# The start and the attention scores of a hybrid decoder trunk: loads, warm-up, split scores, and the place of the last projections

## The chip, the cores and the metric

The kernel runs on one core of a Trainium2 chip. The core has a matrix engine (TensorE, PE in the profile, with its weight loads listed as PEld), VectorE (DVE), ScalarE (ACT), GpSimd (POOL), and a queue engine (SyncE, SP) that issues nearly all DMAs here. Each engine works through its own instructions strictly in the order in which the compiler put them. The metric is the device time of one execution in microseconds (us); lower is better.

## The reference

The input x is 512 tokens by 1024 channels, float32. Two layers follow, each a mixer and a squared-ReLU MLP, each with a residual and a layer norm. Only the mixer of layer 0 is touched by the change:

```python
h = x @ mix_w_in[i] + mix_b_in[i]                    # 1024 -> 2048
u, q, k, v = jnp.split(h, [512, 1024, 1536], axis=-1)
s5_out = s5_mixer(u, ...)                            # diagonal state-space scan, then gelu and a GLU
sb_out = stick_breaking_attention(q, k, v)           # 8 heads of 64, strictly causal
mix = jnp.concatenate([s5_out, sb_out], axis=-1) @ mix_w_out[i] + mix_b_out[i]
...
z = jnp.einsum('bqhd,bkhd->bhqk', q_blk, kf) * scale           # scale = 1/8
log_beta = jax.nn.log_sigmoid(z)
log_keep = jnp.where(strict, jax.nn.log_sigmoid(-z), 0.0)
after = lax.cumsum(log_keep, axis=3, reverse=True) - log_keep
weights = jnp.where(strict, jnp.exp(log_beta + after), 0.0)
out = jnp.einsum('bhqk,bkhd->bqhd', weights, vf)
```

## The kernel before

**Numbers.** Products of weights and activations keep float32 accuracy with operands split in two: hi is the value rounded to F32R, lo is the rest, and `gemm` (L190) forms hi·hi, hi·lo and lo·hi as three F32R products into one PSUM bank. `split` (L185) makes hi with a ScalarE copy and lo with a VectorE subtraction. Some products are still plain F32: the S5 ones, the attention scores (L602) and the weighted sum over the values (L635).

**Weights.** `Weights` (L51) streams 512 KB units: `fetch` issues the load on the SP queue into one of two raw buffers, `_prep` splits the unit into hi (ScalarE, L84) and lo (VectorE, L85) in one of three slots. `next` hands the next unit to a product and splits up to two ahead. The units are listed in the order in which `ORDER` (L48) uses them.

**The start.** The eight 128-channel pieces of x are loaded first (L248), then two weight units (u0 and u1), then the raw S5 tables Braw and Craw and the bias rows. PE first transposes the S5 parameters (`parp`, L276), then each piece of x (L286, four transposes a piece). Each piece is split (`x0h`, `x0l`), and GpSimd adds the halves back to make the residual X (L289). `FIRST` (L45) says behind which pieces the first two weight units are split. Then u0, the first 128 channels of u, is projected by 24 products (L536); eight transposes of Craw (`cp`, L542) are ordered behind its last product; u1 to u3 follow.

**The mixer.** What follows is emitted by the words of `ORDER`: `q0` to `q3` project q, k and v of a pair of heads (`qkv`, L562); `s0` to `s3` build and scan a quarter of the S5 states (`s5_states`, L457); `y0` to `y3` form their outputs; `a0` to `a3` are the attentions of the four pairs; then `gelu` (with a way through DRAM and back, `yf`) and `glu` with its products gg and gv. Last comes `accum` (products acmo, L707), the first half of the output projection. The four sine and cosine tables of the S5 scan (L419 to L435) are all made ahead of `s0`.

**One attention** (L576): v is transposed; the scores of a head stand in three groups A, B and C of key blocks, each in a PSUM bank tagged z (four banks, shared with the S5 products); softplus is Abs, Exp and Ln on ScalarE and one VectorE step, then a GpSimd mask and a split; products with a triangle of ones (L626) sum along the keys; Exp, a mask and the product with v end it. Projections and glu use another three banks (`mm`). The query is scaled by 1/8 when it is copied out of PSUM.

**What sets the order.** The program text gives each instruction a priority (earlier text first, `high_priority` ahead of all), and the compiler's list scheduler puts an engine's instructions in order: in its own simulated time it takes, of those whose operands and buffers are there, the one of best priority. So a projection fills holes of an attention that stands ahead of it in `ORDER`. `add_manual_dep` with NOSYNC and `issue_after` fix an order on one engine without a semaphore. ScalarE's function tables are loaded by `Act` (L116) in the order of the text: a new set is loaded only behind all functions of the old one.

Of the kernel before, what the change touches and what calls it, by code (L numbers as in the profile page):

```python
# [9 lines left out]
F32 = mybir.dt.float32  # L10
F32R = mybir.dt.float32r
# [33 lines left out]
FIRST = (4, 7)  # L45
ATT = "sB0 sC0 wB0 sA0 wC0 sB1 sC1 wB1 sA1 wC1 wA1 wA0"
MIX_BUFS = (3, 4, 1, 4, 3)
ORDER = "q0 s0 q1 y0 s1 a0 y1 s2 q2 y2 s3 a1 y3 gelu q3 a2 glu a3".split()  # L48


class Weights:  # L51
# [23 lines left out]
    def _prep(self, n):  # L75
        nc = self.nc
        while self.done < min(n, len(self.units)):
# [6 lines left out]
            i0 = nc.scalar.copy(hi, raw).ins  # L84
            i1 = nc.vector.tensor_sub(lo, raw, hi.bitcast(F32)).ins  # L85
# [4 lines left out]
            self.done += 1  # L90

# [45 lines left out]
def kernel(ctx: ExitStack, tc: tile.TileContext, a: dict, out: bass.AP):  # L137
# [71 lines left out]
    for o in ORDER:  # L209
        if o[0] == "q":  # L210
            for s in range(1, 4):
                units += units_of("qkv", w_in, 0, 8, [512 * s + 128 * int(o[1])], 128)
# [12 lines left out]
    def zz(name):  # L225
        return psum("z", name, MIX_BUFS[1])
# [16 lines left out]

    xin = []
    with tc.high_priority():
        for j in range(KT):
            xt = att.tile([P, 4, P], F32, tag=("spt", "wt", "q", "k")[j % 4], name=f"xin{j}", bufs=(MIX_BUFS[3], MIX_BUFS[4], 2, 2)[j % 4])
            nc.sync.dma_start(xt, a["x"][0][:, P * j : P * (j + 1)].rearrange("(b p) f -> p b f", p=P))  # L248
            xin.append(xt)
    W = Weights(tc, 2)  # L250
    W.add_slots(wpool, 3)
    W.raw, W.units = s5, units
    W.fetch(0)
# [21 lines left out]
    parp = zz("parp")  # L275
    PE.transpose(parp[:, :96], nat, ident[:96, :96])  # L276
    PE.transpose(parp[:, 96:112], brow, ident[:16, :16])
    par = s5.tile([P, 96], F32, tag="par", name="par")
    V.tensor_copy(par, parp[:, :96])
    V.tensor_copy(PB, parp[:, 96:112])  # L280
    V.tensor_scalar(bq8, PB[:, 4:8], 0.125, None, op0=ALU.mult)
    xs, order = [], []
    for j in range(KT):
        ps = (mm if j % 2 else s5ps)(f"xT{j}")
        for b in range(4):
            PE.transpose(ps[:, b * P : (b + 1) * P], xin[j][:, b, :], ident)  # L286
        xh, xl = page(f"x0h{j}"), page(f"x0l{j}")
        order.append(split(xh, xl, ps))
        G.tensor_tensor(X[j], xh.bitcast(F32), xl.bitcast(F32), op=ALU.add)  # L289
        xs.append((xh, xl))  # L290
    for i, j in enumerate(FIRST):
        W.fence = order[j]
        W._prep(i + 1)
# [126 lines left out]
    for q in range(4):  # L420
# [10 lines left out]
        tc_, ts_ = spage(f"tc{q}", "tabc", 4), spage(f"ts{q}", "tabs", 4)  # L431
# [3 lines left out]
        tabs.append((tc_, ts_))  # L435

# [98 lines left out]
    u0 = mm("u0")  # L535
    u0_last = gemm(u0, W.next(), slice(0, P), xs, 0, T)  # L536
# [25 lines left out]
    def qkv(p):  # L562
        r = []
        for s, n in enumerate("qkv"):
            ps, b = in_proj(4 + 4 * s + p, f"{n}{p}")
            t_ = att.tile([P, T], F32, tag=n, name=f"{n}{p}")
            if s == 0:
                act(t_, ps, AF.Identity, bias=bq8[:, p : p + 1], scale=0.125)
            else:
                act(t_, ps, AF.Identity, bias=b)  # L570
# [569 lines left out]
```

## Time and profile before

| | |
|---|---|
| median of three runs | 1252.57 us (1252.2 to 1254.42) |
| the profiled execution's own time | 1254.81 us |
| its span in the trace | 1252.8 us |
| mean granted PE clock | 0.984 |
| PE busy | 1199.8 us of the span |
| VectorE, ScalarE, GpSimd busy | 778.4, 562.2, 124.3 us |
| first product of u0, first product of u1 | 14.10 us, 23.57 us |
| last product of the mixer (acmo) | 268.38 us |

Times in the rows of the profile count from the span's start. A row of the order of time has the start, the duration, the engine, the line of the kernel, the operation, the tile written and the tiles read, the shape and the count, and, in brackets, the idle time before it with what ended it. A PE record is longer than the distance to the next product, because products are pipelined.

### The profile page before, as it was taken

What the parts mean: (1) busy time and instruction counts of PE and PEld (TensorE: products, weight loads), DVE (VectorE), ACT (ScalarE), POOL (GpSimd) and SP (SyncE); (2) the same over time, 40 slices, a digit from 0 to 9 for tenths busy, and PEclk for the clock granted to TensorE, in tenths of its full rate; (3) what the DMA queues carried; (4) which work ended last, traced back from release to release, by engine and by line L of the source; (5) the groups of instructions that cost most, each with busy time, mean ns of one, the idle gap of its engine ahead of it and who ended that gap; (6) DMA issues with size and microseconds to landing.
All of it is one profiled execution on the core that took longest, in us unless ns stands there. A gap on an engine that the chain in (4) does not pass through costs nothing.

```text
span 1252.8 us, 16561 instructions
## 1 busy us (share of the span) xinstructions
PE 1199.8 (96%) x6503; PEld 1011.9 (81%) x6503; DVE 778.4 (62%) x1313; ACT 562.2 (45%) x1012; POOL 124.3 (10%) x153
## 2 busy tenths in 40 slices
PE   7999989999999999999999999789899999999997
PEld 5886756688988888888998889689898888888885
DVE  8985954567833434434378999999862442444446
ACT  4944476633622313313346576886462331323230
POOL 4002021113000000000030011213500000000000
PEclk9999998999999999999999999889899999999999
DMA  7620121151532222333223221004052242323211
GB/s 183 172 63 17 52 65 45 43 170 32 169 101 101 90 87 92 102 101 101 72 69 102 68 68 35 1 1 135 4 177 90 69 133 67 108 77 118 84 51 68
DMA packets 111662, 105.93 MB, mean 85 GB/s; under 512 B 9378, under 2 KB 99746, under 8 KB 111584
## 3 DMA queue, kind: packets, MB, share of 16 engines
q1 hardware_dynamic: 111424, 104.84, 27.0%
q8 instruction: 51, 0.84, 0.3%
q14 instruction: 27, 0.22, 0.1%
q10 hardware_dynamic: 160, 0.03, 0.0%
HBM read 100.66 MB, written 4.19 MB: 84 GB/s over the span
## 4 chain that ended last, share of the span: by engine, by line
PE 77%; DVE 14%; ACT 5%; issue 1%; POOL 1%; DMA 1%; SPq 0%; DVEq 0%; ACTq 0%; POOLq 0%
PE f L196 23%; PE g L1070 11%; PE acf L196 10%; PE fl L196 4%; PE tlb L196 3%; PE h L1054 3%; DVE cz L312 3%; PE tld L196 3%; PE cv L969 2%; DVE cy L312 2%; PE av L635 2%; DVE wlo L85 2%; PE pl L196 1%; PE q L196 1%; PE acmo L196 1%
## 5 line engine op out<-in xcount | busy, mean ns | idle before, releaser
L84 ACT CAST whi<-raw 128x1024 fp32r<-128x1024 f32 x180 | 188.1, 1049 | 414.3 <-PE f L196 109.4
L85 DVE TENSOR_TENSOR wlo<-raw,whi 128x1024 fp32r<-128x1024 f32 x180 | 226.2, 1260 | 222.8 <-ACT whi L84 222.5
L1070 PE MATMUL g<-whi,hh 128*128 128x512 f32 x208 | 81.5, 392 | 0.0
L1070 PE MATMUL g<-wlo,hh 128*128 128x512 f32 x208 | 81.5, 392 | 0.0
L1070 PE MATMUL g<-whi,hl 128*128 128x512 f32 x208 | 81.4, 391 | 0.0
L196 PE MATMUL f<-xdh,whi 128*128 128x512 f32 x208 | 80.9, 389 | 0.0
L196 PE MATMUL f<-xah,whi 128*128 128x512 f32 x208 | 80.9, 389 | 0.0
L196 PE MATMUL f<-xal,whi 128*128 128x512 f32 x208 | 80.9, 389 | 0.0
L196 PE MATMUL f<-xdh,wlo 128*128 128x512 f32 x208 | 80.9, 389 | 0.0
L196 PE MATMUL f<-xdl,whi 128*128 128x512 f32 x208 | 80.9, 389 | 0.0
L196 PE MATMUL f<-xah,wlo 128*128 128x512 f32 x208 | 80.9, 389 | 0.0
L196 PE MATMUL acf<-hl,whi 128*128 128x512 f32 x192 | 75.2, 392 | 0.0
L196 PE MATMUL acf<-hh,whi 128*128 128x512 f32 x192 | 74.9, 390 | 0.0
L196 PE MATMUL acf<-hh,wlo 128*128 128x512 f32 x192 | 74.7, 389 | 0.0
L186 ACT CAST hh<-fr 128x512 fp32r<-128x512 f32 x64 | 39.7, 621 | 71.6 <-DVE fr L308 71.6
L187 DVE TENSOR_TENSOR hl<-fr,hh 128x512 fp32r<-128x512 f32 x64 | 44.2, 692 | 37.3 <-ACT hh L186 37.3
L312 DVE SCALAR_TENSOR_TENSOR cy<-hp,wdw,cy 128x512 f32<-128x512 f32 (+1 forms) x91 | 60.6, 675 | 0.1
L312 DVE SCALAR_TENSOR_TENSOR cz<-hp,wdw,cz 128x512 f32<-128x512 f32 (+1 forms) x86 | 60.0, 702 | 0.0
L969 PE MATMUL cv<-hph,dh 128*128 128x256 f32 (+1 forms) x113 | 39.9, 353 | 10.3 <-ACT hph L186 8.6
L308 DVE TENSOR_TENSOR fr<-fr 128x512 f32<-128x512 f32 x64 | 43.8, 686 | 5.4 <-ACT fr L125 5.4
L1070 PEld LDWEIGHTS g<-whi,hl 128*128 128x128 f32 x208 | 39.1, 188 | 8.6
L1070 PEld LDWEIGHTS g<-wlo,hh 128*128 128x128 f32 x208 | 39.1, 188 | 8.6
(624 smaller groups left out, 3158.3 us busy)
## 6 DMA issues: line engine op xcount, KB each, us to landing
raw<-in_ffn_w_dram SPq DMA_DIRECT2D x48, 1024.0 KB, 5.2
raw<-in_ffn_w_dram SPq DMA_DIRECT2D x32, 512.0 KB, 3.6
raw<-in_conv_w_pw_dram SPq DMA_DIRECT2D x12, 1024.0 KB, 5.8
raw<-in_mix_w_in_dram SPq DMA_DIRECT2D x16, 512.0 KB, 4.1
xin<-in_x_dram SPq DMA_DIRECT2D x8, 256.0 KB, 4.4
raw<-in_s_w_glu_dram SPq DMA_DIRECT2D x4, 512.0 KB, 3.4
raw<-in_mix_w_out_dram SPq DMA_DIRECT2D x4, 512.0 KB, 3.8
raw<-in_mix_w_out_dram SPq DMA_DIRECT2D x2, 1024.0 KB, 6.2
```

Source lines behind the costliest of these rows:

```text
L84: i0 = nc.scalar.copy(hi, raw).ins
L85: i1 = nc.vector.tensor_sub(lo, raw, hi.bitcast(F32)).ins
L186: i0 = S.copy(hi, src).ins
L187: i1 = V.tensor_sub(lo, src, hi.bitcast(F32)).ins
L196: ins = PE.matmul(ps[:, c0:c1], u[:, k, ksl], v[:, c0:c1], start=start and k == 0 and i == 0, stop=stop and k == n - 1 and i == 2).ins
L308: V.tensor_tensor(o, x, y, op=op)
L312: V.scalar_tensor_tensor(o, x, s, y, op0=op0, op1=op1)
L635: PE.matmul(av[R, P * kb :], vt[:, kb, R], w_[:, o : o + T - P * kb], start=summed[h] == 1, stop=summed[h] == 4, skip_group_check=True)
L969: PE.matmul(cps[j][:, c0:c1], u, v[:, t + c0 : t + c1], start=t == 0 and i == 0, stop=t == n - 1 and i == 2)
L1054: PE.matmul(ps, u, v, start=k == 0 and i == 0, stop=k == nk - 1 and i == 2)
L1070: PE.matmul(pss[b], u, v[:, kk, :], start=k + kk == 0 and i == 0, stop=k + kk == nb - 1 and i == 2)
```

## The change

1. *Loads.* The first weight unit is issued ahead of x; the pieces of x use other buffers.
2. *Warm-up.* 24 transposes of the identity matrix (`WARM`) run on PE ahead of the first piece of x, into the bank of the attention output.
3. *First products.* u0 is no longer projected after all transposes: the three products of piece k are placed behind the transposes of piece k+2. The first weight unit is split with the first piece, the next two behind the last piece. The S5 parameter transposes move behind those of the third piece.
4. *Residual.* X is copied from the transposed PSUM bank by ScalarE; GpSimd no longer adds the halves.
5. *Scores.* q and k are kept as hi and lo, and a score block is three F32R products. The factor 1/8 moves into the split of the q weights. q has two buffers of each half, k one (`QK_BUFS`); before, both had two.
6. *Tables.* The fourth sine table is made behind `y0`, and three buffers hold the tables instead of four.
7. *Order.* `a2` stands ahead of `q3`.

```diff
-FIRST = (4, 7)
+WARM = 24
+QK_BUFS = (2, 1)
-ORDER = "q0 s0 q1 y0 s1 a0 y1 s2 q2 y2 s3 a1 y3 gelu q3 a2 glu a3".split()
+ORDER = "q0 s0 q1 y0 t3 s1 a0 y1 s2 q2 y2 s3 a1 y3 gelu a2 q3 glu a3".split()
...
+            if key[0] == "q":
+                i0 = nc.scalar.mul(hi, raw, 0.125).ins
+                i1 = nc.vector.scalar_tensor_tensor(lo, raw, 0.125, hi.bitcast(F32), op0=ALU.mult, op1=ALU.subtract).ins
...
+    def first(self):
+        self._prep(1)
+        self.got += 1
+        return self.ready.pop(0)
...
+    with tc.high_priority():
+        W.fetch(0)
     xin = []
     with tc.high_priority():
         for j in range(KT):
...
+            tag, bufs = (("spt", MIX_BUFS[3]), ("wt", MIX_BUFS[4]), ("qh", QK_BUFS[0]))[(0, 1, 0, 1, 0, 1, 0, 2)[j]]
...
-    W.fetch(0)
     W.fetch(1)
...
+    warm = psum("av", "warm", MIX_BUFS[2])
+    for i in range(WARM):
+        ready = PE.transpose(warm[:, :P], ident, ident).ins
+    xs, w0, u0 = [], None, mm("u0")
+    def u0_part(k, after):
+        xh, xl = xs[k]
+        for i, (u, v) in enumerate(((w0[0], xh), (w0[0], xl), (w0[1], xh))):
+            ins = PE.matmul(u0, u[:, k], v, start=k == 0 and i == 0, stop=k == KT - 1 and i == 2).ins
+            tc.add_manual_dep(ins, after, NOSYNC, reason="order of the first products")
+            after = ins.name
+        return ins
+    u0_last = ready
     for j in range(KT):
...
+            ins = PE.transpose(ps[:, b * P : (b + 1) * P], xin[j][:, b, :], ident).ins
+            if j == 0 or j > 2:
+                tc.add_manual_dep(ins, u0_last.name, NOSYNC, reason="order of the first products")
         xh, xl = page(f"x0h{j}"), page(f"x0l{j}")
-        order.append(split(xh, xl, ps))
-        G.tensor_tensor(X[j], xh.bitcast(F32), xl.bitcast(F32), op=ALU.add)
+        with tc.high_priority():
+            W.fence = split(xh, xl, ps)
+            if j == 0:
+                W.fence = None
+                w0 = W.first()
+        S.copy(X[j], ps)
         xs.append((xh, xl))
+        if j > 1:
+            u0_last = u0_part(j - 2, ins.name)
+        if j == 2:
+            parp = zz("parp")
...
+    for k in (KT - 2, KT - 1):
+        u0_last = u0_part(k, u0_last.name)
+    W.prep_to(3)
     W.fence = None
...
-    u0 = mm("u0")
-    u0_last = gemm(u0, W.next(), slice(0, P), xs, 0, T)
...
+                t_ = tuple(att.tile([P, T], F32R, tag=n + x, name=f"{n}{x}{p}", bufs=QK_BUFS[s]) for x in "hl")
+                act(t_[0], ps, AF.Identity, bias=b)
+                stt(t_[1], ps, b, t_[0].bitcast(F32), ALU.add, ALU.subtract)
...
-                ins = PE.matmul(z[:, o : o + T - P * kb], k_[R, P * kb : P * kb + P], q_[R, P * kb :], start=o == 0,
-                                stop=True, skip_group_check=True).ins
+                for i, (u, v) in enumerate(((0, 0), (0, 1), (1, 0))):
+                    ins = PE.matmul(z[:, o : o + T - P * kb], k_[u][R, P * kb : P * kb + P], q_[v][R, P * kb :],
+                                    start=o == 0 and i == 0, stop=i == 2, skip_group_check=True).ins
...
+        elif o[0] == "t":
+            tables(int(o[1]))
```

More of the change, by code (lines that the diff above doesn't have):

```diff
@@ L83, in _prep @@
             lo = pool.tile([P, nk, ncol], F32R, tag=f"wlo{s}", name=f"wlo{self.done}", bufs=1)
-            i0 = nc.scalar.copy(hi, raw).ins
-            i1 = nc.vector.tensor_sub(lo, raw, hi.bitcast(F32)).ins
+            if key[0] == "q":
+                i0 = nc.scalar.mul(hi, raw, 0.125).ins
+                i1 = nc.vector.scalar_tensor_tensor(lo, raw, 0.125, hi.bitcast(F32), op0=ALU.mult, op1=ALU.subtract).ins
+            else:
+                i0 = nc.scalar.copy(hi, raw).ins
+                i1 = nc.vector.tensor_sub(lo, raw, hi.bitcast(F32)).ins
             if self.fence:
@@ L419, with tables @@
     tabs = []
-    for q in range(4):
+    def tables(q):
         fa, fb, fr = spage(f"fa{q}"), spage(f"fb{q}"), spage(f"fr{q}")
@@ L435 @@
         tabs.append((tc_, ts_))
+    for q in range(3):
+        tables(q)
     Gx = s5.tile([P, 2, 4, 4, 2, 16], F32, tag="Gx", name="Gx")
```

45 lines of the change are left out of this document (20 added, 25 removed).

## The prediction

> **What bounds the kernel now.** I read the page's busy shares first, then ten-microsecond windows of the mixer stage, then the order of time where a window was poor.
>
> ```profile
> span 1252.8 us, 16561 instructions
> PE 1199.8 (96%) x6503; PEld 1011.9 (81%) x6503; DVE 778.4 (62%) x1313; ACT 562.2 (45%) x1012; POOL 124.3 (10%) x153
> ```
>
> TensorE (PE) is busy for 96% of the span, so time is won only where it has a hole, runs at a low clock, or is given less to do. The diff touches nothing behind the last product of the first mixer:
>
> ```profile
> 268.38 0.39 PE L196 MATMUL acmo<-gh,wlo 128*128 128x512 f32 x1
> ```
>
> Whatever it wins must be won before 268.4 us; the stages behind it move along unchanged.
>
> ```profile
> 10.00:20.00 10.00, 6.75 (x31) 5.28 (x30) 9.93 (x15) 4.56 (x8) 9.29 (x9) 0.85 0.89 175
> 40.00:50.00 10.00, 9.81 (x44) 7.94 (x43) 9.91 (x30) 9.80 (x19) 0.00 (x0) 1.00 0.59 182
> 100.00:110.00 10.00, 8.66 (x34) 5.05 (x34) 5.87 (x12) 5.25 (x12) 1.91 (x4) 0.83 0.15 45
> 140.00:150.00 10.00, 9.70 (x109) 7.39 (x108) 9.85 (x20) 4.95 (x10) 0.00 (x0) 1.00 0.17 55
> 180.00:190.00 10.00, 5.77 (x24) 3.81 (x22) 5.67 (x10) 9.29 (x18) 0.70 (x2) 0.89 0.56 165
> 190.00:200.00 10.00, 10.00 (x42) 8.46 (x42) 4.33 (x7) 4.87 (x11) 1.82 (x4) 0.77 0.37 99
> ```
>
> The columns are the stretch, then busy time of PE, its weight loads, VectorE (DVE), ScalarE (ACT), GpSimd (POOL), the granted clock, DMA share and GB/s. PE has two poor places: the start, and 180 to 190 us, behind which the clock is 0.77. VectorE is full at 40 and at 140 us, so a cost there is not free, and has room at 100.
>
> **Start.** All loads go out on one queue, x ahead of the weights:
>
> ```profile
> 0.80 5.34 SPq L248 DMA_DIRECT2D xin<-in_x_dram  x8
> 13.00 1.04 ACT L84 CAST whi<-raw 128x1024 fp32r<-128x1024 f32 x1 [1.63 <-DMA raw<-in_mix_w_in_dram]
> 18.75 0.63 PE L196 MATMUL u<-x0l,whi 128*128 128x512 f32 x1
> 19.17 0.63 PE L196 MATMUL u<-x0h,wlo 128*128 128x512 f32 x1
> 22.55 0.39 PE L196 MATMUL u<-x0h,wlo 128*128 128x512 f32 x1
> 22.78 1.03 PE L542 MATMUL cp<-ident,Craw 128*128 128x128 f32 x8
> 23.57 0.48 PE L196 MATMUL u<-x0h,whi 128*128 128x512 f32 x1
> 18.00:20.00 2.00, 2.00 (x6) 1.56 (x5) 1.97 (x3) 0.00 (x0) 2.00 (x3) 0.50 0.68 151
> L186 ACT CAST x0h<-xT 128x512 fp32r<-128x512 f32 x8 | 4.4, 588 | 3.8 <-PE xT L286 3.8
> L187 DVE TENSOR_TENSOR x0l<-xT,x0h 128x512 fp32r<-128x512 f32 x8 | 5.1, 678 | 0.0
> L473 ACT COPY gt<-gp 128x512 f32<-128x512 f32 x8 | 4.3, 590 | 9.4 <-PE gp L471 9.4
> ```
>
> Before, the ninth load (the first weights) has landed at 13.00; only then do the 24 products of u0 begin, part of them at a clock of 0.50 (0.42 us apart instead of 0.23), and u1 begins at 23.57. After, the same nine loads run with the weights first, so the last piece of x is there at about 13.0, the bytes being equal. Behind it: four transposes (0.11 each by the 8 in 1.03) 0.45, x0h 0.59, x0l 0.68, handovers about 0.4, the last three products 0.69: 15.8. ACT now also copies each piece to X, 0.59 by the nearest row, so a piece costs it two spacings of about 0.52; the loads spread evenly from 0.8 to 13.0 put the first piece near 5, so eight pieces and one weight split (1.04) end near 14.4, and PE's 1.14 a piece near 14.2, both just in time. I allow 0.6 of lag: u0 ends near 16.4. Then cp (0.8) and u1, whose weights want 1.04 on ACT behind the last x0h and 1.2 on VectorE: 17.3 to 18. I take 18.0 against 23.57: **-5.5**; bounds -7 (no ACT lag) and -1 (first rival). On the queue the first weights now stand ahead of x, and the second weights where they stood. PE's transposes of piece j+2 stand ahead of the products of piece j, so a late piece holds up two pieces' products; with pieces landing some 1.2 apart that is hidden. The parameter transposes (two, 0.7 in all) move behind the third piece, so VectorE's small-step chain starts some 2 us later than before, and gains that back below: 0. The 24 warm-up transposes lie in PE's empty first 6 us, their PSUM bank is not needed before the first attention: 0.
>
> POOL's eight additions to X go. They slow VectorE beside them:
>
> ```profile
> 15.02 5.83 POOL L289 TENSOR_TENSOR X<-x0h,x0l 128x512 f32<-128x512 f32 x4
> 17.71 1.94 DVE L312 SCALAR_TENSOR_TENSOR sm<-sm,sm 128x16 f32<-128x16 f32 x2
> 22.23 0.17 DVE L312 SCALAR_TENSOR_TENSOR sm<-sm,sm 128x16 f32<-128x16 f32 x1
> 19.57 2.36 DVE L85 TENSOR_TENSOR wlo<-raw,whi 128x1024 fp32r<-128x1024 f32 x1
> 24.28 1.22 DVE L85 TENSOR_TENSOR wlo<-raw,whi 128x1024 fp32r<-128x1024 f32 x1 [0.92 <-ACT whi L84]
> ```
>
> A 0.17 us step takes about 1, a 1.22 us one 2.36. Without them VectorE runs some 5 us ahead there. PE, not VectorE, is what later steps wait for up to 90 us, so I count 0, but it is why VectorE follows an earlier start.
>
> **Rounded scores.** A score block was one F32 product (two passes in the trace); now it is three F32R products.
>
> ```profile
> 239.16 0.70 PE L602 MATMUL z3C<-q,k 64*128 64x256 f32 x2
> 241.74 1.12 PE L602 MATMUL z3A<-q,k 64*128 64x512 f32 x2
> 181.25 1.13 PE L602 MATMUL z2B<-q,k 64*128 64x384 f32 x4
> L312 DVE SCALAR_TENSOR_TENSOR yl<-yf,yh 128x512 fp32r<-128x512 f32 x4 | 3.0, 741 | 0.7 <-ACT yh L125 0.6
> ```
>
> A single product's record outlasts its spacing by 0.16 (0.39 against 0.23). So A took 0.96, C 0.54, B 0.97; three passes at 0.227 per 512 columns are 0.68, 0.34, 0.68: -0.28, -0.20, -0.29, twice per attention, -1.5 at most, less where two heads' blocks already ran side by side. In the last two attentions PE is filled with other products and I count -1.4 and -1.1; in the first two the ACT and POOL chain sets the pace: 0. Sum **-2.5**, bounds -5 and +1 (three 64-row weight loads in place of two, 0.1 each where exposed). The low halves are eight more VectorE instructions, 0.74 each by the nearest row, 5.9 in all. For pairs 1 to 3 they can run only when the attention before has released the tiles, behind the first and second attentions' scores, where VectorE has holes; 0, and the third rival if not. ScalarE writes the high halves in the place of the F32 copies: 0. The scaling of the q weights keeps its instruction count: 0. With one k buffer a finished k waits in its PSUM bank until the attention before has made its last scores, which leaves two banks for projections; the copy that waits holds up what stands behind it on ScalarE, the next attention's exponentials at worst, but it is placed behind those scores, which come first on PE too: 0, with the +2 of the next part as its far end. The fourth sine table moves behind y0: on ScalarE and VectorE its 16 instructions need the buffer that the first S5 group gives back, and the first attention's exponentials wait for its sines through the table order. The VectorE steps, by the 0.69 and less of such 512-column work some 2.5 us, fit the hole there,
>
> ```profile
> 79.26 1.23 DVE L85 TENSOR_TENSOR wlo<-raw,whi 128x1024 fp32r<-128x1024 f32 x1 [3.62 <-ACT whi L84]
> ```
>
> 0 again; if the hole is gone, up to +2.5.
>
> **q3 behind the third attention.** The hole it could fill:
>
> ```profile
> 176.28 1.12 DVE L312 SCALAR_TENSOR_TENSOR U<-U,par,yp 128x128 f32<-128x128 f32 x4 [4.79 <-PE yp L523]
> 177.17 0.50 PE L196 MATMUL v<-x0h,whi 128*128 128x512 f32 x1
> 182.22 0.62 ACT L131 ACTIVATE g<-g 128x512 f32<-128x512 f32 x1
> 183.83 1.28 ACT L127 ACT_TABLE_LOAD   x1
> 188.73 0.79 PE L196 MATMUL gg<-yh,whi 128*128 128x512 f32 x1 [4.23 <-ACT yh L125]
> ```
>
> PE waits 4.23 for gelu's result, then runs at a low clock: by the means of 0.89 and 0.77 in the two windows above that costs some 3 more. But the third attention's exponentials need the table load at 183.83, which the code puts behind gelu's last tanh (182.22), and that hangs on the S5 output at 176.28. Putting the attention's scores ahead of v3's products (177.17) starts none of that earlier; the work that is ready before 188 is the same. v3 will also start later, for want of a bank, and so lie in the hole rather than ahead of it. I count half of the clock loss, **-1.5**; bounds -7.2 (hole and clock both gone) and +2 (v3's products wait and displace others).
>
> **Sum:** -5.5 - 2.5 - 1.5 = -9.5. The profiled execution took 1254.81, 2.2 above the median of the runs, so 1245.3 by it, and 1243 against the median of 1252.57.
>
> **The rivals.**
> 1. *The start is lost again.* cp stands behind u0 on PE in program order and needs Craw:
>
> ```profile
> L542 PEldq EVENT_SEMAPHORE  x2: 51/51/51, 17.8 to 19.8; - x2
> ```
>
> Its loads landed by 19.8. If cp is still placed ahead of u1, PE stands from 16.4 to 20 or later and then runs at half clock, as at 18 us above: the start is worth 1 to 2, the sum about -5: 1247.5. Against it: the order is worked out anew and could put u1 first.
> The same end by a page: the Trainium skill, "TensorE: Matmul & The Clock Gate", Part 4 (PE-mode transpose), says that transposes do not count as PE work for the clock, so that the warm-up would do nothing. The trace speaks against that: with nothing but transposes on PE, they went from 7 to 10 in a microsecond.
>
> ```profile
> 8.00:9.00 1.00, 1.00 (x7) 1.00 1.16 310
> 10.00:11.00 1.00, 1.00 (x10) 1.00 1.18 289
> ```
>
> As a mechanism of this kernel: 24 first products 0.42 apart instead of 0.23 cost 4.6 and leave the start about -1, the same 1247.5.
> 2. *The hole closes too.* The attention's scores and v3 interleave so that PE never stands long enough to lose its clock: 5.7 more than the 1.5 counted at most, about -5 more: 1238. The chain through tanh speaks against it.
> 3. *VectorE decides* (the other side). If its full stretches (40 and 140 us above) set the end of the stage, the earlier start is worth nothing and the 5.9 of low halves are paid: +5.9 - 2.5 = +3.4, 1256. It decides once VectorE's last S5 state sum ends no earlier than before. Against it: up to 95 us PE waits for VectorE once,
>
> ```profile
> PE u L196 <- DVE wlo L85: 1.2, 1, 1.2
> ```
>
> and VectorE has the holes at 76 to 79 and at 100 us.
> 4. *Given back at the hole.* The chain to gelu does not move with the start, since it also hangs on lock-ups such as
>
> ```profile
> 157.27 5.68 POOL L595 TENSOR_SCALAR_AFFINE_SELECT sp1B<-sp1B 128x256 f32<-128x256 f32 x1 [0.30 <-DVE sp1B L312]
> ```
>
> and the hole grows by what the start won: about -1.5, 1251.
>
> **How the numbers follow.** Chances: forecast 0.45, rival 1 0.22, rival 2 0.16, rival 3 0.10, rival 4 0.07. Two parts in a thousand, 2.5 us, is what a measurement of this kernel can tell: faster 0.83, same 0.07, slower 0.10. The range 1234 to 1252 takes in the forecast with its unknown costs and the first two rivals and most of the fourth; it leaves out the third and the far end of the second. The forecast's own range is 1238 to 1247.
>
> **What would show it.** u0's last product near 16.4 and u1 near 18 with the clock at 1.00 throughout; VectorE steps of 0.17, not 1, there; cp without a wait. Three score products 0.23 apart. The mixer's last product near 259 instead of 268.4. The wait of gg for yh, if under 4 us, and the clock behind it. Wrong: cp waiting for Craw, a clock of 0.50 in the first products, a wait of a PSUM bank ahead of v3 or gg, the S5 sums ending at 155 as before.

## The result, and the profile after

The changed kernel takes 1259.6 us in the median of its runs, the old one beside it 1254.23: a ratio of 1.0049, 95% interval 1.0031 to 1.0066, so 5.4 us slower by the medians. The prediction was 1243, in a range of 1234 to 1252. All times below are such medians, and all ratios are to the old kernel run beside them; the profiled executions of one kernel scatter by a few us around the median, so single traces are read for places, not for the total.

The page of the changed kernel, span and busy shares:

```profile
span 1255.9 us, 16680 instructions
PE 1203.1 (96%) x6559; PEld 1017.5 (81%) x6559; DVE 777.0 (62%) x1321; ACT 565.1 (45%) x1020; POOL 111.5 (9%) x145
```

TensorE's share is the same, its busy time 3.3 us longer. The order of time on TensorE at the start, and the mixer's last product:

```profile
16.37 0.39 PE L298 MATMUL u<-x0h,wlo 128*128 128x512 f32 x1
18.44 0.63 PE L582 MATMUL cp<-ident,Craw 128*128 128x128 f32 x4 [1.69 <-DMA Craw<-in_s_c_re_dram]
21.15 1.08 PE L582 MATMUL cp<-ident,Craw 128*128 128x128 f32 x4 [2.08 <-DMA Craw<-in_s_c_im_dram]
21.89 0.78 PE L206 MATMUL u<-x0h,whi 128*128 128x512 f32 x1
22.46 0.63 PE L206 MATMUL u<-x0l,whi 128*128 128x512 f32 x1
...
273.55 0.39 PE L206 MATMUL acmo<-gh,wlo 128*128 128x512 f32 x1
```

u0's last product starts at 16.37, just as worked out. Then TensorE stands twice for Craw, because cp comes before u1 in its order, and u1 starts at 21.89, its first products 0.43 apart instead of 0.23. The mixer's last product starts at 273.55; before it was 268.38.

ScalarE, the loads' queue and VectorE behind this, in the order of time (rows left out between them):

```profile
18.05 1.16 ACT L135 ACTIVATE ue<-u,PB 128x512 f32<-128x512 f32 x1
29.46 1.05 ACT L89 CAST whi<-raw 128x1024 fp32r<-128x1024 f32 x1 [10.26 <-DMA raw<-in_mix_w_in_dram]
30.42 0.21 ACT L141 ACTIVATE sm<-sm 128x16 f32<-128x16 f32 x1
...
25.39 1.02 SPq L67 DMA_DIRECT2D raw<-in_mix_w_in_dram  x2
...
30.55 1.23 DVE L90 TENSOR_TENSOR wlo<-raw,whi 128x1024 fp32r<-128x1024 f32 x1 [5.73 <-ACT whi L89]
```

This is the second loss, and the prediction had no line for it. The fourth weights are loaded only at 25.39, behind the bias rows (before, their load went out at 21.96, between the rows). Their high half is next in ScalarE's order, so ScalarE stands 10.26 us, and the small steps towards the sine tables (sm) stand behind it although their inputs are there. VectorE, next in whose order is the low half, stands too:

```profile
20.00:25.00 5.00, 3.85 (x11) 3.23 (x12) 2.87 (x21) 0.00 (x0) 0.00 (x0) 0.50 0.10 22
25.00:30.00 5.00, 5.00 (x20) 4.03 (x19) 0.00 (x0) 0.54 (x1) 0.00 (x0) 0.82 0.72 195
150.00:160.00 10.00, 7.63 (x38) 5.99 (x37) 10.00 (x17) 9.25 (x19) 3.39 (x4) 1.00 0.01 2
180.00:190.00 10.00, 7.26 (x39) 5.57 (x37) 6.96 (x13) 9.73 (x19) 0.65 (x2) 1.00 0.36 92
190.00:200.00 10.00, 7.82 (x33) 6.39 (x34) 4.31 (x8) 4.83 (x10) 0.70 (x2) 0.83 0.49 146
```

The columns are those of the prediction's windows. From 25 to 30 us VectorE does nothing at all. Further on, TensorE is busy 7.63 of the ten from 150 to 160 (9.19 before), and from 180 to 200 it does 15.08 where it did 15.77: the old hole in front of gg is not closed but split, as two waits of TensorE from 150 to 210 us show (total, times, longest):

```profile
PE gg L206 <- ACT yh L135: 2.2, 1, 2.2
PE z2B L670 <- ACT sh2B L196: 1.9, 1, 1.9
```

What is missing from 150 to 160 is told by the products of v for the fourth pair of heads (v3 in the prediction) between 140 and 200 us, first and last start, before (line 196) and after (line 206):

```profile
L196 PE MATMUL v<-x0h,whi x8: 387/391/499, 155.7 to 180.0; 128*128 128x512 f32 x8
...
L206 PE MATMUL v<-x0h,whi x8: 389/391/397, 168.7 to 186.0; 128*128 128x512 f32 x8
```

Before, v3 began at 155.7 and filled the gaps of the second attention. Now it begins at 168.7. Up to that attention's scores nothing is lost (147.7 now, 147.4 before): the whole loss of the mixer arises behind them. Some of the expectations below call this tile v2.

### The profile page after: what moved, and what is told of

Read it like the earlier page. It is cut to its first block, busy times and chain, and to the rows that moved or that the text cites. A ratio compares the mean times of both kernels' runs of the same rounds, so it can differ in the third digit from the quotient of the medians.

```text
span 1255.9 us, 16680 instructions
## 1 busy us (share of the span) xinstructions
PE 1203.1 (96%) x6559; PEld 1017.5 (81%) x6559; DVE 777.0 (62%) x1321; ACT 565.1 (45%) x1020; POOL 111.5 (9%) x145
## 4 chain that ended last, share of the span: by engine, by line
PE 71%; DVE 15%; issue 6%; ACT 4%; DMA 2%; SPq 1%; POOL 1%; DVEq 0%; POOLq 0%; ACTq 0%
PE f L206 23%; PE g L1116 11%; PE acf L206 10%; PE fl L206 4%; PE h L1100 3%; PE tld L206 3%; DVE cz L350 3%; PE tlb L206 2%; PE cv L1015 2%; DVE wlo L90 2%; DVE cy L350 2%; PE av L679 2%; PE acmo L206 1%; PE pl L206 1%; PE pv L206 1%
## 5 line engine op out<-in xcount | busy, mean ns | idle before, releaser
L89 ACT CAST whi<-raw 128x1024 fp32r<-128x1024 f32 x176 | 183.8, 1049 | 409.4 <-PE f L206 111.3
L90 DVE TENSOR_TENSOR wlo<-raw,whi 128x1024 fp32r<-128x1024 f32 x176 | 219.4, 1250 | 222.9 <-ACT whi L89 222.3
```

## The experiments

Each run's ratio is to the old kernel on the same chip; in the same terms the changed kernel stands at 1.0049 (1.0031 to 1.0066). Diffs are against the changed kernel unless another is named.

### First four: one part undone at a time

**cp behind u1.**

```diff
-    with tc.issue_after(u0_last):
-        for i in range(2):
-            cp = zz(f"cp{i}")
...
     for j in range(4):
         ps, b = in_proj(j, f"u{j}") if j else (u0, pv("mix_b_in", 0))
+        if j == 1:
+            with tc.issue_after(last[0]):          # u1's last product
+                for i in range(2):
+                    cp = zz(f"cp{i}")
...
```

> The changed kernel with one edit: the eight transposes of Craw (cp) are emitted behind u1's 24 products instead of ahead of them. Theory S (the start's gain is lost because cp, in its old place ahead of u1, waits on TensorE for Craw, which lands at about 21, and the clock then drops to half): u1's first product comes at 17.5 to 18.5 instead of 21.89, all its products are 0.23 apart, u1 ends near 24 instead of 29.8, and the kernel is 3 to 5.5 us faster than the changed one, near 1255. It can be cut to some 3 by the weights of u3, whose load is now issued only at 25.4, behind the bias rows. Rival (VectorE or the attention chain sets the pace of the stage): u1 comes as early, but the mixer's last product stays within 1 us of 273.5 and so does the time of 1259.6.

In this kernel the moved block's loop variable overwrote u1's bias, so u1 is computed with another bias; the work is the same. Measured: 1263.11, ratio 1.0074 (1.0059 to 1.0089), 3 us slower still. u1's first product came at 16.50 at full clock, as expected; but ScalarE's load wait stayed, at 30.23, and VectorE's waits (second row: total and longest) grew:

```profile
30.23 1.04 ACT L89 CAST whi<-raw 128x1024 fp32r<-128x1024 f32 x1 [8.56 <-DMA raw<-in_mix_w_in_dram]
...
DVE wlo L90 <- ACT whi L89: 10.4, 2, 8.3
```

The first S5 state Sx came at 74.1 instead of 71.7. Theory S alone falls: TensorE's early start runs into the missing weights, for which it now stood 2.27 us at 31.33.

**The old order.**

```diff
-ORDER = "... y3 gelu a2 q3 glu a3".split()
+ORDER = "... y3 gelu q3 a2 glu a3".split()
```

> The changed kernel with q3 put back ahead of a2 in ORDER, nothing else. Theory O (the swap costs: y3's products, the third attention and v3 fall behind each other from 160 us on, where the changed kernel falls from 0.5 to 3.5 us behind the old one): the third attention's sums and gg move back, gg's first product comes near 189.5 instead of 192.2, the mixer's last product at 270 to 271 instead of 273.5, and the kernel is 2 to 3.5 us faster, near 1256.5. Rival (the three passes of the scores and their low halves cost it, wherever q3 stands): the time stays within 1 us of 1259.6.

Measured: 1258.39, 1.0033 (1.0020 to 1.0045). 1 to 2 us faster, the intervals overlapping; the swap is not the main cost. gg's first product came later (194.6), not earlier, so the reason given was wrong too.

**The old start.** Loads, transposes, u0 and X as in the old kernel, with x's eight pieces in the buffers that the changed kernel leaves free.

```diff
-    with tc.high_priority():
-        W.fetch(0)
     xin = []
...
+    W.fetch(0)
     W.fetch(1)
...
-        S.copy(X[j], ps)
+        G.tensor_tensor(X[j], xh.bitcast(F32), xl.bitcast(F32), op=ALU.add)
...
-        if j > 1:
-            u0_last = u0_part(j - 2, ins.name)
...
+    u0 = mm("u0")
+    u0_last = gemm(u0, W.next(), slice(0, P), xs, 0, T)
```

> The changed kernel with the old start (x ahead of the weights on the queue, no warm-up transposes, u0 behind all transposes, X added on GpSimd), the rest of the change kept. Theory S (the new start as it stands is worth nothing): 1259 to 1260.5, u1's end within 1 us of the old 29.0. Rival (the new start wins 3 or more in VectorE's and GpSimd's work, which other parts then lose): 1262 or more. Other rival (the new start itself costs, through late loads): 1257 or less.

Measured: 1258.33, 1.0027 (1.0014 to 1.0040), in none of the three expected ranges, and u1's end at 27.1 instead of 29.0. The new start as built wins nothing; with overlapping intervals, it may cost up to 3.

**F32 scores.**

```diff
-                t_ = tuple(att.tile([P, T], F32R, tag=n + x, ..., bufs=QK_BUFS[s]) for x in "hl")
-                act(t_[0], ps, AF.Identity, bias=b)
-                stt(t_[1], ps, b, t_[0].bitcast(F32), ALU.add, ALU.subtract)
+            t_ = att.tile([P, T], F32, tag="qkv"[s] + ("h" if s == 0 else ""), name=f"{n}{p}")
+            act(t_, ps, AF.Identity, bias=b if s else bq8[:, p : p + 1])
...
-                for i, (u, v) in enumerate(((0, 0), (0, 1), (1, 0))):
+                ins = PE.matmul(z[:, o : o + T - P * kb], k_[R, P * kb : P * kb + P], q_[R, P * kb :], start=o == 0, stop=True, ...).ins
```

> The changed kernel with the scores as one F32 product again, q and k as F32 tiles with two buffers each, no low halves; start, order and the late fourth table kept. Theory R (the rounded scores cost more than they win: one k buffer keeps a finished k in its PSUM bank, eight more VectorE instructions): 2 to 4 us faster, near 1256.5, with the old 9.2 us of TensorE work between 150 and 160 us back. Rival (the scores win what was counted, 2.5, and the swap costs it all): 1261 to 1262.5.

Measured: 1254.44, 1.0008 (0.9995 to 1.0020): 5 us faster than the changed kernel, and the old time again. The rounded scores with their single k buffer, counted together as a gain of 2.5, carry the whole loss. The mixer's last product came at 268.8.

### The score's parts

**Only the high halves, with one and with two buffers for k.**

```diff
-                t_ = tuple(att.tile([P, T], F32R, tag=n + x, ...) for x in "hl")
+                t_ = [att.tile([P, T], F32R, tag=n + "h", ..., bufs=QK_BUFS[s])]
                 act(t_[0], ps, AF.Identity, bias=b)
-                stt(t_[1], ps, b, t_[0].bitcast(F32), ALU.add, ALU.subtract)
...
-                for i, (u, v) in enumerate(((0, 0), (0, 1), (1, 0))):
+                for i, (u, v) in enumerate(((0, 0),)):
...
-QK_BUFS = (2, 1)
+QK_BUFS = (2, 2)      # the second kernel only
```

> The changed kernel with only the high halves' product of the scores: the low halves of q and k and the two products with them are left out (the output is less exact), k still has one buffer. Theory D (VectorE's eight low halves and the added passes cost): as fast as the kernel with F32 scores or faster, 1252 to 1255, 5 to 7 under the changed kernel. Theory K (the single k buffer, which holds a finished k in its PSUM bank until the attention before has made its last scores, costs): 1257 or more, and the next kernel with two k buffers is at least 2 faster.

> The same with two buffers for k, which the space of the left-out low halves allows. Theory K: 2 to 4 us faster than with one buffer. Theory D: within 1 us of it.

Measured: 1251.23, 0.9984 (0.9975 to 0.9992), and 1247.02, 0.9938 (0.9923 to 0.9954). The first number alone would have fitted theory D; the pair shows that the second k buffer is worth 4 us there. v3's first product came at 164.3 with one buffer and at 151.2 with two.

**One k buffer in the old kernel.**

```diff
# against the old kernel
-            t_ = att.tile([P, T], F32, tag=n, name=f"{n}{p}")
+            t_ = att.tile([P, T], F32, tag=n, name=f"{n}{p}", bufs=(2, 1, 2)[s])
```

> The old kernel with one buffer for k (F32) instead of two, and x's pieces in other buffers of the same pool, since two of them used k's; nothing else. Theory K (a finished k waits in its PSUM bank for the attention before, so that the next v's products do not fill the attention's hole): 3 to 5 us slower than the old kernel, 1257 to 1259, v2's first product near 168 instead of 155.7, TensorE busy under 8 of the 10 us from 150 to 160 instead of 9.2. Rival (k's one buffer only hurts together with the low halves): within 1 us of the old kernel.

Measured: 1259.31, 1.0032 (1.0019 to 1.0045). Only k's second buffer was taken (and x's pieces, two of which had used it, lie in other buffers), and the old kernel loses 4 to 5 us in the place named. The rows of v3 and the window there; then the copy of the third pair's k out of its PSUM bank, in the old kernel and in this one:

```profile
L196 PE MATMUL v<-x0h,whi x8: 390/394/496, 167.9 to 181.6; 128*128 128x512 f32 x8
...
150.00:160.00 10.00, 7.80 (x38) 5.96 (x37) 10.00 (x18) 8.95 (x19) 3.80 (x4) 1.00 0.00 1
...
127.99 0.69 ACT L125 ACTIVATE k<-k,PB 128x512 f32<-128x512 f32 x1
...
166.21 0.69 ACT L125 ACTIVATE k<-k,PB 128x512 f32<-128x512 f32 x1 [0.23 <-PE z1A L602]
```

With one buffer the third pair's k, whose products were done near 122, is copied out only at 166.21, behind the last scores of the second attention (z1A). Until then it holds one of the three projection banks; q and k of the fourth pair wait in the other two, as they do in the old kernel. So v3 has no bank before that copy, and starts at 167.9. In the changed kernel the copy comes at 166.87 and v3 at 168.7.

**Two k buffers in the changed kernel.**

```diff
-MIX_BUFS = (3, 4, 1, 4, 3)
-QK_BUFS = (2, 1)
+MIX_BUFS = (3, 4, 1, 3, 3)
+QK_BUFS = (2, 2)
-        vt = att.tile([P, 4, P], F32, tag="vt", name=f"vt{p}")
+        vt = att.tile([P, 4, P], F32, tag="vt", name=f"vt{p}", bufs=1)
```

> The changed kernel with two buffers for the halves of k; the space comes from one buffer fewer for the scores' exponentials (three) and for the transposed v (one), which can only cost. Theory K: at least 2 us faster than the changed kernel, 1255 to 1257.5, v2's first product near 156. Rival: 1259 or more.

Measured: 1258.27, 1.0032 (1.0021 to 1.0044): 1 to 2 us, under the 2 expected, intervals overlapping; v3's first product came at 160.3, between the old place and the new. In the full kernel the second buffer did not give the 4 back. That the late start and the low halves lie over it is a guess that this run does not show; the space taken from the other tiles could cost here as well.

### The start, freed

**Bias rows behind the u projections,** alone and with cp behind u1.

```diff
-    rows = s5.tile([P, 2, P], F32, tag="sp", name="rows", bufs=6)
-    G.memset(rows, 0.0)
-    for n in vecs:
...
     for j in range(4):
         ps, b = in_proj(j, f"u{j}") if j else (u0, pv("mix_b_in", 0))
...
+    rows = s5.tile([P, 2, P], F32, tag="sp", name="rows", bufs=6)
+    G.memset(rows, 0.0)
+    for n in vecs:
...
     pvp = zz("pvp")
```

> The changed kernel with the loads of the bias rows (and the transposes that use them) emitted behind the u projections, so that the fourth and fifth weights' loads no longer stand behind them on the queue (25.39 before). cp stays ahead of u1. Theory Q (the early start is lost on the loads' queue: ScalarE stands 10.26 us for the fourth weights, behind that wait stand the sine tables' first steps, and VectorE stands idle from 23 to 30 and then is full to 70, so that the first S5 states, not TensorE, set what follows): ScalarE's wait shrinks to under 4 us, VectorE is busy over 6 of the 10 us from 20 to 30, the first Sx comes at 65 to 68 instead of 71.7, TensorE's 1.3 us of waits for Cx at 57 go, and the kernel is 1.5 to 4 us faster than the changed one. Theory S (only cp's wait and the clock behind it count): within 1 us of the changed one, although VectorE is earlier.

> Both edits: the bias rows' loads behind the u projections and cp behind u1. If Q and S are both needed (with cp alone moved, VectorE stood even longer, for the loads), now u1 starts near 18 at full clock, u ends at 35 to 36 instead of 40.4, the first gp near 52.5 instead of 57.2, and the kernel is 4 to 6 us faster than the changed one, 1253.5 to 1255.5. Rival (the middle of the stage is paced by VectorE and the attention chain, whatever the start): as e5 within 1 us.

Measured: 1259.98, 1.0048 (1.0036 to 1.0061), no change, and 1257.83, 1.0027 (1.0015 to 1.0039). In the first, VectorE was busy 6.0 of the ten from 20 to 30, just as expected, but ScalarE still waited 4.87 us, the first gp moved from 57.2 to 61.4, behind products of q1, and the first Sx to 76.5: a miss. In the second, u ended at 34.1 instead of 40.4, 6.3 earlier, but the first gp came at 57.5, not near 52.5; the gain was lost again at 50 to 60 us, where the transposes of the bias rows (pvp) now stood for their own loads:

```profile
PE pvp L602 <- DMA rows<-in_conv_b_pw_dram: 3.7, 1, 3.7
```

**Those transposes far back** (both moved to just ahead of the second attention), with rounded and with F32 scores.

```diff
     for o in ORDER:
+        if o == "a1":
+            bias_rows()
```

Here bias_rows holds the rows' 14 loads, pvp and the copy to PV.

> The changed kernel with cp behind u1 and with both the bias rows' loads and the transposes that use them moved far back, to just ahead of the second attention (in the run before, those transposes stood on TensorE for their loads 3.7 us at 50 to 60 us and gave back the 6.3 us that u had won). Theory Q+S (the new start is good for what was predicted, once no load and no transpose stands in front of ready work): u ends near 34, the first gp comes near 52, the first Sx near 66 to 67, and the kernel is 4 to 6 us faster than the changed one, 1253.5 to 1255.5, ratio to the old near 1.000. Rival (VectorE and the attention chain pace what follows): the first Sx at 70 or later, or the second attention's scores still at 146 or later, and 1257 or more.

> The same with the scores as one F32 product, q and k in two F32 buffers each. If the freed start and the two k buffers add up (4 to 6 and about 4 to 5 under the changed kernel): 1249 to 1251, 3 to 5 us faster than the old kernel. Rival (the attention's hole takes back what comes early, as with the freed start in the run before): 1253 to 1255.

Measured: 1263.53, 1.0070 (1.0057 to 1.0084), and 1262.06, 1.0065 (1.0050 to 1.0079). Up to the first attention all went as expected in the first of them (first gp 51.2, first Sx 65.7, first scores 83.3, each some 6 early). Then the loads, moved back with the transposes, were late again. The wait, and the windows there:

```profile
PE pvp L728 <- DMA rows<-in_ffn_b_dram: 7.6, 1, 7.6
...
150.00:160.00 10.00, 3.07 (x12) 2.77 (x13) 6.16 (x11) 2.49 (x5) 0.31 (x1) 0.69 0.21 64
160.00:170.00 10.00, 8.77 (x30) 6.96 (x30) 4.71 (x14) 8.16 (x17) 2.01 (x6) 0.50 0.01 2
170.00:180.00 10.00, 10.00 (x36) 7.31 (x35) 3.89 (x7) 5.03 (x11) 0.58 (x2) 0.61 0.00 0
```

The two runs say nothing against the start. They show what a transpose that nobody needs yet costs when it stands in TensorE's order ahead of its load.

**Loads early, transposes late.** cp behind u1, the rows' loads behind the u projections, the transposes behind the first S5 outputs; then the same with F32 scores; then also with the old order.

```diff
+    rows = load_rows()           # behind the u projections
...
     for o in ORDER:
+        if o == "s1":
+            bias_rows()
```

> The changed kernel with cp behind u1, the bias rows' loads behind the u projections, and the transposes that use them behind the first S5 outputs, near 75, by when their loads (landed by 61 in the run with both edits) are long there. Theory Q+S: no wait of these transposes; u ends near 34, first gp near 51.5, first Sx near 66, first attention's scores near 83.5, and the kernel is 3 to 6 us faster than the changed one, 1253.5 to 1256.5. Rival (the middle takes it back): the second attention's scores at 146 or later although the first ones come near 84, and 1258 or more.

> The same with the scores as one F32 product and two F32 buffers for q and k. If they add: 1249 to 1251.5, ratio to the old kernel 0.996 to 0.998. Rival (the hole takes it back): 1253.5 to 1255.

> The same once more with q3 ahead of a2: of the change only the freed start and the late fourth table are left. Theory O (the swap costs about 1): 1248 to 1251, up to 1.5 us faster than with the swap. Rival (the swap gains what was counted, 1.5): 1.5 slower than with it. The old kernel's time, 1253.5 to 1255, would mean that the start cannot be won at all.

Measured: 1254.12, 0.9994 (0.9982 to 1.0006); 1248.53, 0.9946 (0.9930 to 0.9963), a little faster than expected; 1249.48, 0.9961 (0.9945 to 0.9977). The start of the first, on TensorE, then the windows from 20 to 30 and ScalarE's wait for the fourth weights:

```profile
16.50 0.39 PE L286 MATMUL u<-x0h,wlo 128*128 128x512 f32 x1
16.73 0.40 PE L206 MATMUL u<-x0h,whi 128*128 128x512 f32 x1
...
22.82 1.03 PE L576 MATMUL cp<-ident,Craw 128*128 128x128 f32 x8
...
20.00:25.00 5.00, 5.00 (x28) 4.23 (x27) 3.00 (x29) 2.27 (x7) 0.00 (x0) 1.00 1.02 272
25.00:30.00 5.00, 5.00 (x24) 4.12 (x23) 4.86 (x16) 4.93 (x14) 0.00 (x0) 1.00 0.23 64
...
24.02 1.05 ACT L89 CAST whi<-raw 128x1024 fp32r<-128x1024 f32 x1 [2.31 <-DMA raw<-in_mix_w_in_dram]
```

u1 follows u0 without a gap, cp waits for nothing, the clock stays at 1.00 and VectorE is at work from 25 on. 1259.6 to 1254.12 is 5.5 us (7 by the ratios), but that is against the broken start; against the old start with the rest of the change (1258.33) it is 4, and the third kernel, which has of the change little more than the freed start, is 4 to 5 faster than the old one. The freed start also holds three things that the change does not have: the later place of cp, of the rows' loads and of their transposes. They were not tried with the old start, so how much of the 4 to 5 is theirs alone is open; cp, for one, waited for nothing in the old kernel. With F32 scores the kernel is 5.7 us faster than the old one, the best of the versions here that form the whole scores. The old order is 1 us slower than the new one there, with overlapping intervals.

### The rounded scores, with the freed start

One k buffer with F32 scores; rounded scores with two k buffers (space taken as above); F32 scores with the same space taken.

```diff
# e19, against the freed start with F32 scores
-  t_ = att.tile([P, T], F32, tag=..., name=f"{n}{p}")
+  t_ = att.tile([P, T], F32, tag=..., name=f"{n}{p}", bufs=(2, 1, 2)[s])
# e20: QK_BUFS = (2, 2); e20 and e21: MIX_BUFS[3] = 3, vt with bufs=1
```

> The freed start with F32 scores and the new order (1248.53 before), but one buffer for k. Theory K (the single buffer is nearly all of the 5.6 us between F32 and rounded scores): 1252 to 1254. Theory D (VectorE's low halves and the passes cost it): 1248 to 1250.

> The freed start with rounded scores and two buffers for the halves of k, with three buffers instead of four for the exponentials and one for the transposed v. Theory K: 1249 to 1252, and within 1.5 us of the next kernel. Theory D: 1253 to 1255, and 3 us or more above the next kernel. The prediction's term would be 2.5 us below the next kernel.

> The freed start with F32 scores and two k buffers, the same space taken as in the kernel before: 1248.5 to 1250.5; the excess over 1248.53 is the price of the taken space.

Measured: 1254.14, 0.9999 (0.9989 to 1.0009); 1252.65, 0.9989 (0.9979 to 0.9998); 1249.66, 0.9964 (0.9952 to 0.9976). So the single k buffer costs 5.6 us in the F32 kernel, as theory K had it, and the rounding alone, with two buffers, costs 3.0 where a gain of 2.5 was counted: the second number lies between the two theories, nearer to D. (The two do not add: rounded with one buffer is 5.6 above F32 with two.) For the first: v3's products, with two buffers (first start 149.8) and with one, and the windows of the hole:

```profile
L206 PE MATMUL v<-x0h,whi x8: 389/392/398, 149.8 to 178.4; 128*128 128x512 f32 x8
...
145.00:155.00 10.00, 9.38 (x46) 7.24 (x45) 10.00 (x18) 8.29 (x17) 4.71 (x4) 1.00 0.04 10
```

```profile
L206 PE MATMUL v<-x0h,whi x8: 389/389/628, 164.1 to 182.8; 128*128 128x512 f32 x8
...
145.00:155.00 10.00, 6.92 (x32) 5.64 (x30) 10.00 (x19) 7.86 (x16) 4.79 (x4) 0.86 0.12 36
155.00:165.00 10.00, 9.93 (x24) 5.63 (x24) 3.03 (x7) 4.67 (x10) 2.74 (x4) 0.50 0.05 18
```

A late v3 is not dear by itself. In the third kernel, with two buffers but less space, it begins at 160.8 and the time is only 1.1 us above 1248.53; there the fourth pair's k fills the gap, TensorE's longest wait is 0.9 us and its clock stays at 1.00. With one buffer it stands 3.1 us in two waits between 149.6 and 153.2, and then runs at half clock to 166: that is where the time goes.

For the second, the rounding. The first Sx comes at 66.8 with rounded scores and at 63.1 with F32 scores in the same space, because in the first TensorE waits 2.83 us for the first group's Cx, which stands in VectorE's order behind the low halves of pair 0:

```profile
PE tp L509 <- DVE Cx L338: 2.8, 1, 2.8
...
53.58 0.74 DVE L338 SCALAR_TENSOR_TENSOR kl<-k,PB,kh 128x512 fp32r<-128x512 f32 x1
54.33 0.49 DVE L338 SCALAR_TENSOR_TENSOR Cx<-cm 64x320 f32<-64x320 f32 x1
```

But this delay does not last: the first scores are at 86.8 and 83.2, the second at 144.3 and 144.2. The two kernels part again in the second attention: the third attention's first scores are at 177.2 and 173.1, the mixer's last product at 267.4 and 265.5. Seen there: the three products of one score block no longer run as a group. In the second head's block C two start near 159.5, the last at 162.69, behind products of the weighted sum that wait 1.34 us for GpSimd, and so the block's softplus is late (rounded, then F32 scores):

```profile
163.11 0.38 ACT L135 ACTIVATE sp1C<-z1C 128x256 f32<-128x256 f32 x1 [2.07 <-PE z1C L647]
...
157.26 0.38 ACT L135 ACTIVATE sp1C<-z1C 128x256 f32<-128x256 f32 x1
```

Whether this makes up the 3.0 us was not tried; its cause stays open.

The marks of the stage, from the traces (us; "v3" is the first product of the fourth pair's v, "end" the start of the mixer's last product):

| kernel | u1 first | u last | Sx first | 1st scores | 2nd scores | v3 | end | ratio |
|---|---|---|---|---|---|---|---|---|
| before | 23.6 | 39.8 | 70.8 | 87.6 | 147.4 | 155.7 | 268.4 | 1 |
| changed | 21.9 | 40.4 | 71.7 | 89.3 | 147.7 | 168.7 | 273.5 | 1.0049 |
| F32 scores | 23.6 | 41.2 | 72.4 | 90.8 | 148.8 | 157.3 | 268.8 | 1.0008 |
| start freed | 16.7 | 34.4 | 63.8 | 83.9 | 143.5 | 165.6 | 269.1 | 0.9994 |
| freed, F32 | 16.5 | 34.1 | 63.1 | 83.2 | 141.3 | 149.8 | 261.2 | 0.9946 |
| freed, F32, one k | 16.5 | 34.1 | 63.0 | 83.0 | 141.4 | 164.1 | 267.4 | 0.9999 |

The last two rows are alike up to the second scores at 141 and then part by 6 us: that is the k buffer alone. The first four columns show the start's gain carried through VectorE's full stretch.

## Why the prediction was wrong, step by step

- **The end of u0** (16.4): right, 16.37. Of the steps behind it the trace shows TensorE just in time: from 6.55 to 16.76 it stands for no piece longer than 0.27 us. VectorE's small steps take 0.17, as the prediction's signs had it. There was luck in the 23.57 that it was compared with: it held the half clock of one trace, and in two later runs with the old start u1 comes at 21.75 and 22.17. Some 1.4 to 1.8 of the 5.5 rested on that.
- **"Then cp (0.8) and u1":** this step failed. cp was given its own time and no wait, with u1 at 18.0; it waited 1.69 and 2.08 us for Craw and u1 came at 21.89, at half clock. The first rival named exactly this, and had been given 0.22 because the order "could put u1 first". It was priced too mildly as well: against the old start (1258.33) the new one was worth nothing, not 1 to 2.
- **"the second weights where they stood":** here the queue was followed one load too short. The fourth weights, behind the rows, held ScalarE for 10.26 us and with it VectorE; no part of the sum and no rival had it. The run with cp alone moved shows that mending the failed step above by itself makes things worse. With both mended, and the rows' transposes out of the way, the start is worth 4 to 5.5 (4 against the old start, 5.5 by the medians against the broken one), part of which may belong to those two repairs. So a start freed of both waits is worth nearly what was summed; that the change brings it was wrong.
- **The first rival's other half:** the Trainium skill, "TensorE: Matmul & The Clock Gate", Part 4 (PE-mode transpose), says that transposes do not count as PE work for the clock. The trace disagrees: with only transposes before, their spacing fell from 0.21 to 0.11 near 6.4 us, and u0's first products were 0.23 apart, the full-clock spacing. In the old kernel the same step from 0.21 to 0.11 comes near 10 us, also with only transposes before.

```profile
1.57 5.13 PE L290 MATMUL warm<-ident 128*128 128x128 f32 x24 [1.57 <-POOL ident masks.py:199]
6.55 1.88 PE L307 MATMUL xT<-ident,xin 128*128 128x128 f32 x12
10.18 0.39 PE L298 MATMUL u<-x0l,whi 128*128 128x512 f32 x1
10.41 0.39 PE L298 MATMUL u<-x0h,wlo 128*128 128x512 f32 x1
```

- **Rounded scores, -2.5:** measured +5 with the single k buffer. Three entries of this part were wrong. The gain itself did not come: 512-column products are 0.23 apart, as counted, but the old blocks were already quicker than their records less 0.16. Block A took 0.65, not 0.96; and block B of three products took 0.91, not 0.68. The first four blocks of the second attention (B, C, A, B) with the first product behind them, before and after:

```profile
147.40 1.13 PE L602 MATMUL z1B<-q,k 64*128 64x384 f32 x4
150.52 0.50 PE L196 MATMUL k<-x0h,wlo 128*128 128x512 f32 x1
...
147.69 0.44 PE L646 MATMUL z1B<-qh,kh 64*128 64x384 f32 x1
150.75 0.50 PE L206 MATMUL k<-x0h,wlo 128*128 128x512 f32 x1
```

They take 3.12 and 3.06 us, a gain of 0.06 where 1.06 was counted. "With one k buffer a finished k waits in its PSUM bank": the bank was seen, its price was set at 0 with +2 as the far end; it is 4 to 5 alone in the old kernel and 5.6 with the freed start. What was priced was the waiting copy on ScalarE. What costs is the filler: v3 gets no bank until the second attention has made its last scores, TensorE has nothing to fill that attention with, stands, and loses its clock. The bound of +1 on the whole part was thus too small. "The low halves ... 0": they were placed for pairs 1 to 3; pair 0's stand at 46 to 54 us, where the window quoted for 40 to 50 already showed VectorE full at 9.91. They delay the first Sx, but that delay is gone by the second scores; what makes the rounding cost 3.0 with two k buffers stays open.
- **q3 behind a2, -1.5:** not resolved. Undone, the changed kernel is 1 to 2 us faster; undone in the freed F32 kernel, 1 slower; both with overlapping intervals. "v3 will also start later, for want of a bank, and so lie in the hole": right (it ran until 186.4), but it was counted only as good for the hole at 180. That it was what filled the second attention from 155 on was overlooked. The hole was split, not closed; 180 to 200 us hold 0.7 less TensorE work than before. From 180 to 210 the clock was 1.00, 0.83 and 0.83 (0.89, 0.77 and 1.00 before), so by these means the half of the clock loss that was counted as won did not come.
- **The fourth sine table, 0:** not tried alone. The freed start with F32 scores and the old order still has it, and stands at 4 to 5 us faster than the old kernel, so start, late table and scaled weights together are worth that; no run separates them.
- **The signs:** of those for being wrong, cp waiting for Craw, a clock of 0.50 in the first products (u1's) and the S5 sums ending as before (154.7; 154.4 then) came true, and v3 got its bank 13 us later.
- **The rivals:** the third (VectorE decides, 1256) came nearest in time, and its sign came true. Its reason does not hold: with the start freed, low halves included, the last S5 sum ends at 150.6. The measured 1259.6 lies beyond all of them.

By the measured terms, the start 0 instead of -5.5, the scores with one k buffer +5 instead of -2.5, and the swap within 2 of 0 give about +5, against +5.4 measured. These are differences of single runs that need not add, as the k buffer and the rounding show.

## What to carry to other kernels

When work is pulled forward, follow every in-order queue past it until the next thing that is not ready: here the transposes of Craw on TensorE and one weight load on the loads' queue stood in the way of a gain of 4 to 5, and curing the first alone made the second worse. A buffer count is a schedule: ask which later product needs the bank that a waiting result holds, and what that product was filling; an item with no consumer in sight costs its whole wait, and the clock behind it, if it stands ahead of its load (9.4 us between the two places of the bias rows' loads and transposes). A zero in a sum needs its cover named for each instance, the first one too.

## What the runs showed of the hardware

A hole cost more than its length, through the clock. In the kernel whose bias transposes stood 7.6 us, the granted clock was 0.50 from 154 to 177 us, although TensorE is shown busy without a break from 166 on; it came back with the v products, which begin at 176.3 there. Two of its windows:

```profile
170.00:174.00 4.00, 4.00 (x11) 2.14 (x9) 0.24 (x1) 1.05 (x3) 0.00 (x0) 0.50 0.00 0
178.00:180.00 2.00, 2.00 (x14) 1.83 (x14) 1.18 (x3) 0.82 (x3) 0.29 (x1) 1.00 0.00 0
```

With one k buffer in the freed F32 kernel it was 0.50 from 155 to 165 with TensorE busy 9.93 of the ten (window above). In the changed kernel's start, where projection products follow the wait that ends at 21.15, they were 0.23 apart again from 26.8 on. The Trainium skill, "TensorE: Matmul & The Clock Gate", Part 1 (The HAM clock gate), puts the return at some 3.4 us of sustained work; the start's 5.7 us are within about twice that, the attention's stretches are not. In them TensorE ran attention products; whether their kind, or short gaps that the records hide, keep the clock down was not tried.
